# A decoder layer's down projection as seven block products, with its sums made ahead

## The chip, the cores and the metric

One core of one Trainium2 chip runs one decoder layer in single precision. The metric is device time in microseconds for one execution. Engines are named as the profile names them: PE (matrix engine; PEld is its weight load), DVE (vector), ACT (scalar), POOL (GpSimd), SP (the queue that issues nearly all transfers).

## The reference

The layer has a mixer (stick-breaking attention beside gated linear attention), a normalisation, a gated feed-forward with a causal convolution of width 3, and a second normalisation. The change concerns the last product and what follows it:

```python
def conv_glu_ffn(h, w_ff_gate, w_ff_up, conv_w, conv_b, w_down):
    ...
    return (jax.nn.silu(conv) * up) @ w_down          # (2048, 2816) @ (2816, 1024)
...
y = conv_glu_ffn(h, ...)
x = layer_norm(DEEPNORM_ALPHA * x + (1.0 + gate_f) * y, ln2_g, ln2_b)
```

## The kernel before, in words

The 2048 tokens are four tiles of 512 (`TQ`), each of four blocks of 128 (`NB`). A single-precision product is made from three fast matmuls: each operand is split into a rounded part "hi" and a rest "lo", and hi·hi, hi·lo and lo·hi are accumulated. ACT makes the hi part (a cast), DVE or POOL the lo part (a subtraction).

The program has these stages in the order in which they run. The **mixer** (`projections`, `attend`, `gla`, `mixer_out`) mixes PE work with long DVE scans (line 541), POOL products (543) and masks (532, 534). Small left-over jobs are spread over it by `with_ada` (854): a list `ada_todo` of 24 items, one after every fourth yield of `between(t)`; they load through the three buffers `w_raw` of the ring pool. The **feed-forward products** gate and up (`unit`, 1038) use one level of Strassen's form over pairs of token tiles (`t2` = 0 or 1): per unit seven products of 12 matmuls, two column blocks of 128 at a time (index `fp`), 40 units in all and four plain column pairs (`plain`, 1111). The up unit multiplies its result into the gated tile `cv` (two buffers), on POOL for three of the four quarters (1059) and on DVE for one (1078), and stores each half to the DRAM tile `da` (1093). The next gate unit then takes the two `cv` buffers again for its convolution on DVE (1106 to 1108).

The **down projection** (1195 to 1227) is plain: two halves of 512 output columns, in each all 16 token blocks, in each 22 row blocks of 128, and three matmuls for each (`row_wide`, 412). The activations of a block come from `da` one block ahead (`load_a`, 1179), in three parts that go around the buffer pairs `pl`, `gt`, `wsum`, `cv`; the weights of a half stay in the tiles that held the feed-forward's operands. After the first half, the gated sum goes to DRAM (`dr0`) and comes back in the second, where `norm` (383) finishes the rows.

The order on every engine is set by a scheduler that walks the program by priority; `act`, `dve` and `pool` (104) are wrappers that put an operation 300 places ahead. Each engine then runs its list strictly in order.

## Time and profile before

| | us |
|---|---|
| median of 3 runs (2945.28 to 2954.65) | 2952.74 |
| the profiled execution's own time | 2947.66 |
| its span in the profile | 2946.0 |
| busy: PE / DVE / ACT / POOL | 2746.0 / 2013.4 / 1107.6 / 1028.1 |

The span is what lies between the first and the last instruction; the execution's own time has 1.66 us around it. In the stages at the end PE is busy in nearly every slice, DVE about half to three quarters, and POOL stops altogether when the down projection begins.

### The profile page before, as it was taken

How to read it: one execution, taken by the hardware profiler on the slowest of the kernel's cores; microseconds unless marked ns; L12 is line 12 of the kernel's file. 1: busy time of each engine (PE TensorE's matmuls, PEld its weight loads, DVE VectorE, ACT ScalarE, POOL GpSimd, SP SyncE). 2: the span in 40 equal slices, each digit the busy share in tenths (PEclk: the TensorE clock that was granted, in tenths of full speed). 3: DMA queues.
4: the chain of work that ended last, by engine and by line, in shares of the span. 5: the costliest groups of instructions: out<-in, count | busy, mean ns of one | idle time of the engine just before them, and what ended most of it. 6: DMA issues, size and time to landing. Idle time of an engine off the chain costs nothing. (4 is left out here: it accounts for less than half of the span.)

```text
span 2946.0 us, 38134 instructions
## 1 busy us (share of the span) xinstructions
PE 2746.0 (93%) x13387; PEld 2219.7 (75%) x13387; DVE 2013.4 (68%) x2841; ACT 1107.6 (38%) x1870; POOL 1028.1 (35%) x1139
## 2 busy tenths in 40 slices
PE   7989999989999998978979999989999998999998
PEld 6867887777788775656757887867888886888887
DVE  6475567578887789798667767686766665335665
ACT  2442244365656556434223332243223233112111
POOL 2550222155444346375463436462333341000000
PEclk9999999999999998989889999999999999999999
DMA  8978775757684455556784454353322236445553
GB/s 308 361 252 277 256 248 195 229 199 233 204 258 148 143 165 160 172 170 229 265 314 157 122 158 150 115 165 115 86 80 86 79 106 232 130 133 184 167 164 114
DMA packets 370424, 539.62 MB, mean 183 GB/s; under 512 B 25182, under 2 KB 224056, under 8 KB 370232
## 3 DMA queue, kind: packets, MB, share of 16 engines
q1 hardware_dynamic: 368504, 530.89, 55.8%
q0 software_dynamic: 1728, 6.29, 0.6%
q8 instruction: 106, 1.74, 0.2%
q14 instruction: 86, 0.70, 0.1%
HBM read 404.82 MB, written 132.26 MB: 182 GB/s over the span
## 5 line engine op out<-in xcount | busy, mean ns | idle before, releaser
L541 DVE TENSOR_TENSOR_SCAN pp<-pp,beta 128x512 f32<-128x512 f32 (+2 forms) x320 | 384.8, 1218 | 66.4 <-POOL beta L534 37.0
L543 POOL TENSOR_TENSOR beta<-beta,pp 128x512 f32<-128x512 f32 (+2 forms) x160 | 206.2, 1289 | 349.4 <-DVE pp L541 275.0
L101 POOL TENSOR_TENSOR w_lo<-wsum,w_hi 128x1024 fp32r<-128x1024 f32 x80 | 208.2, 2602 | 173.8 <-ACT w_hi L101 173.7
L1017 PE MATMUL acc<-t,w_lo 128*128 128x512 f32 x640 | 247.0, 392 | 9.4 <-DVE w_lo L101 9.3
L1015 PE MATMUL acc<-t,w_hi 128*128 128x512 f32 x640 | 250.2, 393 | 4.4 <-ACT k L1073 2.8
L1016 PE MATMUL acc<-t,w_hi 128*128 128x512 f32 x640 | 249.8, 390 | 0.0
L556 DVE TENSOR_TENSOR wl<-wt,wh 128x512 fp32r<-128x512 f32 (+1 forms) x320 | 186.7, 598 | 82.0 <-ACT wh L555 81.6
L555 ACT CAST wh<-wt 128x512 fp32r<-128x512 f32 (+1 forms) x320 | 162.6, 530 | 201.8 <-PE wt L551 185.9
L529 ACT ACTIVATE pp<-z 128x512 f32<-128x512 f32 (+2 forms) x320 | 173.7, 544 | 121.2 <-PE z L528 81.9
L101 ACT CAST w_hi<-w_raw 128x512 fp32r<-128x512 f32 (+2 forms) x173 | 125.5, 747 | 245.8 <-PE acc L1016 63.6
L292 PE MATMUL acc<-hh,w_hi 128*128 128x512 f32 x480 | 194.5, 406 | 3.8 <-DVE st L101 3.0
L551 PE MATMUL wt<-ident,beta 128*128 128x128 f32 x1088 | 184.2, 286 | 13.8 <-DVE beta L543 8.5
L293 PE MATMUL acc<-hl,w_hi 128*128 128x512 f32 x480 | 192.1, 401 | 0.5 <-DVE hl L101 0.5
L294 PE MATMUL acc<-hh,w_lo 128*128 128x512 f32 x480 | 191.7, 400 | 0.6 <-POOL w_lo L101 0.6
L530 ACT ACTIVATE beta<-z 128x512 f32<-128x512 f32 (+2 forms) x320 | 171.0, 543 | 15.2 <-PE wt L551 15.2
L559 PE MATMUL o_ps<-wl,v 128*128 128x512 f32 (+1 forms) x320 | 133.7, 422 | 43.6 <-DVE wl L556 41.4
L551 PEld LDWEIGHTS wt<-ident,beta 128*128 128x128 f32 x1088 | 139.7, 147 | 44.5 <-DVE beta L543 11.9
L101 DVE TENSOR_TENSOR w_lo<-w_raw,w_hi 128x512 fp32r<-128x512 f32 (+1 forms) x140 | 136.8, 1000 | 53.1 <-ACT w_hi L101 27.5
L527 PE MATMUL z<-k,q 128*128 128x512 f32 (+2 forms) x320 | 137.9, 434 | 16.5 <-ACT beta L530 14.1
L301 PE MATMUL acc<-w_hi,hh 128*128 128x256 f32 (+1 forms) x512 | 148.5, 290 | 1.4 <-ACT w_hi L101 0.7
L1017 PEld LDWEIGHTS acc<-t,w_lo 128*128 128x128 f32 x640 | 120.5, 188 | 37.7 <-DVE w_lo L101 12.3
L302 PE MATMUL acc<-w_lo,hh 128*128 128x256 f32 (+1 forms) x512 | 147.7, 289 | 0.9 <-POOL w_lo L101 0.9
(332 smaller groups left out, 7260.0 us busy)
## 6 DMA issues: line engine op xcount, KB each, us to landing
w_raw<-in_w_ff_gate_dram SPq DMA_DIRECT2D x48, 512.0 KB
w_raw<-in_w_ff_up_dram SPq DMA_DIRECT2D x48, 512.0 KB
k<-dk SPq DMA_DIRECT2D x160, 128.0 KB
v<-dv SPq DMA_DIRECT2D x80, 256.0 KB
da<-cv SPq DMA_DIRECT2D x40, 512.0 KB
w_hi<-dwi_0h SPq DMA_DIRECT2D x39, 512.0 KB
w_lo<-dwi_0l SPq DMA_DIRECT2D x39, 512.0 KB
q<-dq SPq DMA_DIRECT2D x128, 128.0 KB
```

The source lines that it names most:

```text
L101: return f(*args, **kw)
L292: nc.tensor.matmul(ps, hi[:, k % 4, cs], xh[k], start=(k == 0), stop=False)
L293: nc.tensor.matmul(ps, hi[:, k % 4, cs], xl[k], start=False, stop=False)
L294: nc.tensor.matmul(ps, lo[:, k % 4, cs], xh[k], start=False, stop=(k == nk - 1))
L529: nc.scalar.activation(pp[:, 0:n], z[:, 0:n], AF.Sigmoid, scale=-1.0)
L541: nc.vector.tensor_tensor_scan(pp[:, 0:n][:, ::-1], pp[:, 0:n][:, ::-1], beta[:, 0:n], first, ALU.mult, ALU.bypass)
L543: (nc.gpsimd if i in PMU and jt < PMJ else nc.vector).tensor_mul(beta[:, 0:n], beta[:, 0:n], pp[:, 1:n + 1])
L551: pe.transpose(wt[:, i * P:(i + 1) * P], ws[i][:, ks], ident)
L556: nc.vector.tensor_sub(wl[:, cs], wt[:, cs], wh[:, cs])
L1015: nc.tensor.matmul(ps, w[0][:, k, :], t[k][:, 0, :], start=first and k == 0, stop=False, **add)
L1016: nc.tensor.matmul(ps, w[0][:, k, :], t[k][:, 1, :], start=False, stop=False, **add)
L1017: nc.tensor.matmul(ps, w[1][:, k, :], t[k][:, 0, :], start=False, stop=k == 3, **add)
```

## The change

The down projection too is done in one level of Strassen's form. A pair of blocks (block `b` of token tiles 2·t2 and 2·t2+1) gives the two row halves, odd and even row blocks of the weight the two inner halves, and the two halves of 512 columns the two column halves. Eight pairs of blocks and seven products give 56 steps of 11 × 3 matmuls. The products run one after another, each over all eight pairs (`steps`). The results are put together on DVE and ACT in eight tiles `top` (the ring's weight tiles) and eight tiles `low` (operand tiles), so that `dr0` goes.

- **Weight sums.** `sum_w_down(k)`, eleven items at the end of `ada_todo`, taken every second yield: two loads of 512 KB into `w_raw`, three stores of quarters, four POOL subtractions of 128x512 in place, four stores.
- **Activation sums.** `act_sums` after every up unit: four POOL additions or subtractions of 128x512 in the two `cv` tiles, in place, so after their stores to `da`; then four stores to the new DRAM tile `dsa`. The two column pairs that are done by `plain` for the first pair of token tiles are read back and summed by `plain_sums` during later units.
- **Down projection.** Weights come unsplit from DRAM, 11 tiles of 128x512 per product, through 17 tile places; activations come in two parts of 6 and 5 row blocks.

```diff
+    def sum_w_down(k):
+        q = []
+        for j in range(2):
+            raw = wring.tile([P, 1024], F32, name="w_raw", bufs=3)
+            nc.sync.dma_start(raw, w_down[(2 * k + j) * P:(2 * k + j + 1) * P, :])
+            q += [raw[:, 0:512], raw[:, 512:]]
+        b11, b12, b21, b22 = q
+        for d, x in zip(dws[k][4:], (b11, b21, b22)):
+            nc.sync.dma_start(d, x)
+        nc.gpsimd.tensor_sub(b11, b12, b11)
+        nc.gpsimd.tensor_sub(b12, b22, b12)
+        nc.gpsimd.tensor_sub(b22, b22, b11)
+        nc.gpsimd.tensor_sub(b21, b21, b22)
+        for d, x in zip(dws[k], (b11, b12, b22, b21)):
+            nc.sync.dma_start(d, x)
...
-            if cs and i >= ADA0 and i % ADAE == ADAE - 1:
+            n = ADAE if len(cs) > NH else 2
+            if cs and i >= ADA0 and i % n == n - 1:
...
+    ada_todo += [partial(sum_w_down, k) for k in range(NH)]
...
+        if up:
+            act_sums(t2, fp, dst[0][:, A], dst[1][:, A], dst[0][:, B], dst[1][:, B])
+
+    def act_sums(t2, fp, a11, a12, a21, a22):
+        nc.gpsimd.tensor_add(a22, a21, a22)
+        nc.gpsimd.tensor_sub(a21, a11, a21)
+        nc.gpsimd.tensor_sub(a11, a22, a11)
+        nc.gpsimd.tensor_sub(a12, a12, a11)
+        for j, x in enumerate((a22, a11, a21, a12)):
+            nc.sync.dma_start(dsa[t2][:, :, j, fp], x.rearrange("p (b c) -> p b c", c=P))
...
+    def load_w(i, k):
+        w = t_tile(*slots[n_w[0] % NW])
+        n_w[0] += 1
+        raw = w[:, 1, :].bitcast(F32)
+        nc.sync.dma_start(raw, products[i][0](k))
+        act.copy(w[:, 0, :], raw)
+        dve.tensor_sub(w[:, 1, :], raw, w[:, 0, :])
+        return w
...
+    def finish(r, blk, ps, last):
+        t = small()
+        nc.vector.tensor_mul(t, ps, gfb[:, 0:512])
+        nc.vector.tensor_add(r[:, 0:512], r[:, 0:512], t)
+        stats(r, blk, 0)
+        dst = out[blk * P:(blk + 1) * P, :]
+        norm(r, st_all[:, blk], g2b, b2b, nc.vector, m1, (dst[:, 0:512], dst[:, 512:D]) if last else (dst,))
...
+    steps = [(i, b) for i in range(7) for b in range(NP2)]
...
+    for s, (i, b) in enumerate(steps):
+        xh, xl = ahead.pop()
+        if s + 1 < len(steps):
+            ahead.append(load_a(*steps[s + 1]))
+        ps = psm.tile([P, TQ], F32, name="acc", bufs=3)
+        for k in range(NH):
+            w = wset[i][k]
+            nc.tensor.matmul(ps, xh[k], w[:, 0, :], start=k == 0, stop=False)
+            nc.tensor.matmul(ps, xh[k], w[:, 1, :], start=False, stop=False)
+            nc.tensor.matmul(ps, xl[k], w[:, 0, :], start=False, stop=k == NH - 1)
+        if i < 6:
+            if 0 < b < NW - NH + 1:
+                wset[i + 1].append(load_w(i + 1, b - 1))
+            elif b == NP2 - 1:
+                wset[i + 1] += [load_w(i + 1, k) for k in range(NW - NH, NH)]
+        r, blk = top[b], b // NB * 2 * NB + b % NB
+        if i == 0:
+            nc.scalar.copy(r[:, L], ps)
+        elif i == 1:
+            low.append(wide(NW + b))
+            nc.vector.tensor_add(low[b][:, L], r[:, L], ps)
+            nc.scalar.copy(r[:, R], low[b][:, L])
+            gated(r, blk, 0)
+        elif i == 2:
+            nc.vector.tensor_add(low[b][:, L], low[b][:, L], ps)
+        elif i == 3:
+            nc.vector.tensor_add(r[:, R], r[:, R], ps)
+            nc.vector.tensor_add(low[b][:, R], low[b][:, L], ps)
+            gated(low[b], blk + NB, 1)
+            stats(low[b], blk + NB, 1)
+            gated(low[b], blk + NB, 0)
+        elif i == 4:
+            finish(low[b], blk + NB, ps, False)
+        elif i == 5:
+            nc.vector.tensor_add(r[:, R], r[:, R], ps)
+            gated(r, blk, 1)
+            stats(r, blk, 1)
+        else:
+            finish(r, blk, ps, s + 1 == len(steps))
```

(`gated` loads 256 KB of the first normalisation's result, multiplies by the gate and adds: two DVE operations of 128x512; `stats` is one.)

The scheduler moves the instructions. The first place is POOL between two up units of the second pair of token tiles; lines 1059 and 1085 are the product into `cv`, `w_lo<-wsum` makes the lo part of a summed feed-forward weight, 1047 and 1073 copy two columns. Before, three rows of weight work stand behind the last product of a unit:

```order
L1059 TENSOR_TENSOR cv<-cv,k_22150 128x512
L101 TENSOR_TENSOR w_lo<-wsum,w_hi 128x1024
L1059 TENSOR_TENSOR cv<-cv,k_22173 128x512
L101 TENSOR_TENSOR w_lo<-wsum,w_hi 128x1024 x2
L1047 COPY gt<-halo 128x2 x2
L101 TENSOR_TENSOR w_lo<-wsum,w_hi 128x1024
```

And now (1133 to 1136 are the four sums):

```order
L102 TENSOR_TENSOR w_lo<-wsum,w_hi 128x1024
L1085 TENSOR_TENSOR cv<-cv,k_21725 128x512
L1133 TENSOR_TENSOR cv<-cv 128x512
L1134 TENSOR_TENSOR cv<-cv 128x512
L102 TENSOR_TENSOR w_lo<-wsum,w_hi 128x1024
L1135 TENSOR_TENSOR cv<-cv 128x512
L1136 TENSOR_TENSOR cv<-cv 128x512
L102 TENSOR_TENSOR w_lo<-wsum,w_hi 128x1024
L1073 COPY gt<-halo 128x2 x2
```

Two sums stand between the last product and the first of those weight rows, and two behind it.

The second place is POOL in the mixer, in the stage of the third token tile (543 and 565 are the attention's products). Before:

```order
L540 COPY pp<-pp 128x1
L543 TENSOR_TENSOR beta<-beta,pp 128x512
L540 COPY pp<-pp 128x1 x2
L543 TENSOR_TENSOR beta<-beta,pp 128x512
L540 COPY pp<-pp 128x1 x2
L543 TENSOR_TENSOR beta<-beta,pp 128x512
```

And now, at the same place:

```order
L565 TENSOR_TENSOR beta<-beta,pp 128x512
L562 COPY pp<-pp 128x1
L359 TENSOR_TENSOR w_raw<-w_raw 128x512
L360 TENSOR_TENSOR w_raw<-w_raw 128x512
L562 COPY pp<-pp 128x1
L565 TENSOR_TENSOR beta<-beta,pp 128x512
L562 COPY pp<-pp 128x1 x2
```

The weight sums (359 to 362) stand one or two at a time between the attention's rows; all 44 lie between the places of the rows that start at about 834 and 1078 us in the trace of before.

The third place is PE where the down projection begins: the row at which it first needs the buffer pair `cv`. Before:

```order
L420 MATMUL acc_22799<-t5_1_22773,wsum_22708 128x512
L421 MATMUL acc_22799<-t5_0_22772,wsum_22707 128x512
L419 MATMUL acc_22888<-t0_0_22712,cv_22785 128x512
L420 MATMUL acc_22888<-t0_1_22713,cv_22785 128x512
L421 MATMUL acc_22888<-t0_0_22712,cv_22784 128x512
```

And now:

```order
L1306 MATMUL acc_23383<-t1_2_23147,wsum_23330 128x512
L1307 MATMUL acc_23383<-t1_2_23147,wsum_23330 128x512
L1306 MATMUL acc_23236<-t1_2_23147,cv_23187 128x512
L1307 MATMUL acc_23236<-t1_2_23147,cv_23187 128x512
L1308 MATMUL acc_23383<-t1_2_23147,wsum_23329 128x512
L1306 MATMUL acc_23383<-t1_3_23151,wsum_23330 128x512
```

Before, 41 matmuls of the down projection stand between the last one of the feed-forward and this place; now 93 do, because the first parts of later steps (those in `pl`, `wsum` and `gt`) are put ahead.

## Rows read from the trace of the kernel before

**Rows 1.** The page: span, and busy time by engine.

```profile
span 2946.0 us, 38134 instructions
PE 2746.0 (93%) x13387; PEld 2219.7 (75%) x13387; DVE 2013.4 (68%) x2841; ACT 1107.6 (38%) x1870; POOL 1028.1 (35%) x1139
```

**Rows 2.** Windows (stretch, length, busy us by engine, clock, DMA): feed-forward, then both halves.

```profile
2060.00:2440.00 380.00, 376.71 (x1658) 310.69 (x1657) 265.38 (x306) 117.21 (x153) 146.79 (x86) 1.00 0.31 90
2500.00:2600.00 100.00, 100.00 (x443) 82.83 (x442) 36.57 (x41) 19.51 (x20) 0.00 (x0) 1.00 0.45 134
2800.00:2935.00 135.00, 135.00 (x598) 111.81 (x597) 84.93 (x169) 24.30 (x25) 0.00 (x0) 1.00 0.45 145
```

**Rows 3.** Timeline (start, us, engine, line; idle before): the down projection's beginning.

```profile
2453.74 1.28 POOL L1059 TENSOR_TENSOR cv<-cv,k 128x512 f32<-128x512 f32 x1 [3.37 <-DVE k L1058]
2456.47 0.59 SPq L1093 DMA_DIRECT2D da<-cv  x1
2460.86 0.34 SPq L1188 DMA_DIRECT2D cv<-da  x1
2467.97 1.04 ACT L101 CAST cv<-cv 128x1024 fp32r<-128x1024 f32 x1 [0.51 <-DMA cv<-da]
2469.07 0.79 PE L419 MATMUL acc<-t,cv 128*128 128x512 f32 x1 [10.08 <-ACT cv L101]
```

**Rows 4.** Timeline: one load of activations in the first half, issue and cast.

```profile
2561.44 0.32 SPq L1188 DMA_DIRECT2D pl<-da  x1
2565.30 1.05 ACT L101 CAST pl<-pl 128x1024 fp32r<-128x1024 f32 x1 [3.84 <-DMA pl<-da]
```

**Rows 5.** Timeline: DVE for one block of the second half, first to last operation.

```profile
2800.81 0.96 DVE L101 TENSOR_TENSOR cv<-cv 128x768 fp32r<-128x768 f32 x1 [3.79 <-ACT cv L101]
2801.68 0.69 DVE L1220 TENSOR_TENSOR t<-acc,t 128x512 f32<-128x512 f32 x1
...
2805.57 1.23 DVE L101 TENSOR_TENSOR pl<-pl 128x1024 fp32r<-128x1024 f32 x1
...
2808.47 1.29 DVE L395 SCALAR_TENSOR_TENSOR t<-t,rn_rs,t 128x1024 f32<-128x1024 f32 x1
```

**Rows 6.** Timeline: from an up unit's last product to the next convolution.

```profile
2100.90 1.67 POOL L1059 TENSOR_TENSOR cv<-cv,k 128x512 f32<-128x512 f32 x1 [2.00 <-DVE k L1058]
2102.60 0.52 SPq L1093 DMA_DIRECT2D da<-cv  x1
2117.14 0.75 DVE L1106 TENSOR_SCALAR cv<-gt,ccols 128x1024 f32<-128x1024 f32 x1
2117.30 2.85 POOL L101 TENSOR_TENSOR w_lo<-wsum,w_hi 128x1024 fp32r<-128x1024 f32 x1 [6.39 <-ACT w_hi L101]
2117.93 3.31 DVE L1107 SCALAR_TENSOR_TENSOR cv<-gt,ccols,cv 128x1024 f32<-128x1024 f32 x1
2122.95 0.68 DVE L101 TENSOR_TENSOR w_lo<-w_raw,w_hi 128x512 fp32r<-128x512 f32 x1
2130.51 0.50 PE L1017 MATMUL acc<-t,w_lo 128*128 128x512 f32 x1 [0.82 <-DVE w_lo L101]
```

**Rows 7.** Source lines 1107 and 1058, feed-forward of the second pair: ns minimum/median/maximum.

```profile
L1107 DVE SCALAR_TENSOR_TENSOR cv<-gt,ccols,cv x20: 1275/2290/3310, 2076.4 to 2437.0; 128x1024 f32<-128x1024 f32 x20
L1058 DVE TENSOR_TENSOR k<-k,acc x19: 680/687/689, 2062.2 to 2409.3; 128x512 f32<-128x512 f32 x19
```

**Rows 8.** Windows of the mixer: two stretches.

```profile
690.00:830.00 140.00, 132.53 (x773) 107.01 (x773) 120.97 (x157) 82.02 (x165) 69.29 (x109) 0.99 0.71 233
834.00:1078.00 244.00, 232.43 (x1375) 192.00 (x1374) 186.35 (x250) 142.11 (x276) 99.05 (x161) 0.99 0.51 163
```

**Rows 9.** Groups by line: POOL's attention product, 850 to 1110 us.

```profile
L543 POOL TENSOR_TENSOR beta<-beta,pp 128x512 f32<-128x512 f32 x29 | 48.6, 1674 | 98.6 <-DVE pp L541 72.1 <-PE wt L551 8.3 <-PE o_ps L557 4.6
```

**Rows 10.** Timeline: the end, PE's last matmul and the DVE operation behind it.

```profile
2935.21 0.39 PE L421 MATMUL acc<-t,cv 128*128 128x512 f32 x1
2935.63 0.69 DVE L1220 TENSOR_TENSOR t<-acc,t 128x512 f32<-128x512 f32 x1 [7.41 <-PE acc L421]
```

More of the change, by code (lines that the diff above doesn't have):

```diff
@@ L1171, in t_pair, with pairs @@
-    def t_pair(i):
-        return [t_tile(*slots[2 * i + j]).rearrange("p k c -> p (k c)") for j in range(2)]
-    wd = [[], []]
-    for n in range(first, len(units)):
-        unit(n, (0, 1, 3, 4, 2, 5, 6) if n == first else range(7))
-    n_a = [0]
-    def load_a(b):
+    wide = lambda n: t_tile(*slots[n]).rearrange("p k c -> p (k c)").bitcast(F32)
+    def pairs():
+        return [x[:, 512 * i:512 * (i + 1)] for x in
+                [ft.tile([P, WIDTH["pl"]], F32, name="pl", bufs=2) for _ in range(2)] for i in range(2)]
@@ L1181, in load_a @@
+    n_w, n_a = [0], [0]
+    def load_w(i, k):
[6 more added lines that the diff above has]
+        return w
+    def load_a(i, b):
         hi, lo = [], []
-        for f0 in range(0, NFF, 8):
-            n = min(8, NFF - f0)
-            pool, name = ((ft, "pl"), (right["ft2"], "gt"), (ft, "wsum"), (right["ft2"], "cv"))[n_a[0] % 4]
+        src = products[i][1](b)
+        for f0, n in PARTS:
+            pool, name = ((ft, "pl"), (ft, "wsum"), (right["ft2"], "gt"), (right["ft2"], "cv"))[n_a[0] % 4]
@@ L1193, in load_a, with gated @@
         return hi, lo
-    ahead = [load_a(0)]
-    wd[0] += [load_down(0, i, t_pair(i)) for i in range(NFF // 2)]
-    gfb, g2b, b2b = rows = [t_tile(*slots[22 + i]).rearrange("p k c -> p (k c)").bitcast(F32) for i in range(3)]
+    def gated(r, blk, half):
+        ds = slice(half * 512, (half + 1) * 512)
+        x1 = small()
+        nc.sync.dma_start(x1, dx1[blk // NB][blk % NB][:, ds])
+        nc.vector.tensor_mul(r[:, ds], r[:, ds], gfb[:, ds])
+        nc.vector.scalar_tensor_tensor(r[:, ds], x1, ALPHA, r[:, ds], ALU.mult, ALU.add)
@@ new lines, in stats @@
+    def stats(r, blk, half):
+        nc.vector.bn_stats(st_all[:, blk, half, :], r[:, half * 512:(half + 1) * 512])
+    def finish(r, blk, ps, last):
[5 more added lines that the diff above has]
+        norm(r, st_all[:, blk], g2b, b2b, nc.vector, m1, (dst[:, 0:512], dst[:, 512:D]) if last else (dst,))
+    wsums = plain_sums()
+    for n in range(first, len(units)):
+        unit(n, (0, 1, 3, 4, 2, 5, 6) if n == first else range(7))
+        if n >= first + 2:
+            next(wsums, None)
@@ L1198, in layer @@
+    run(wsums)
+    steps = [(i, b) for i in range(7) for b in range(NP2)]
+    ahead = [load_a(0, 0)]
+    wset = [[load_w(0, k) for k in range(NH)]] + [[] for _ in range(7)]
+    gfb, g2b, b2b = rows = [wide(25 + i) for i in range(3)]
     for d, src in zip(rows, (dgate[1], ln2_g, ln2_b)):
         nc.sync.dma_start(d, src.to_broadcast([P, D]))
[L1200 to L1227 removed]
@@ new lines, in layer @@
+    top = [w.bitcast(F32) for _ in range(NP2 // 2) for w in ring_pair()]
+    low = []
+    L, R = slice(0, 512), slice(512, D)
+    for s, (i, b) in enumerate(steps):
[37 more added lines that the diff above has]
+            finish(r, blk, ps, s + 1 == len(steps))
```

72 lines of the change are left out of this document (32 added, 40 removed).

## Prediction

> **What bounds the kernel now.** I read the page's first lines, then the windows of the stages that the change touches, and last the timeline at the places where a buffer changes hands.
>
> The page says that PE is busy 93% of the span and no other engine over 68% [rows 1]. An average hides the stages, so the windows come next [rows 2]. The reader is to see three things. In a stretch of each half of the down projection PE never rests: 443 matmuls in 100 us, 0.2257 us each, at a granted clock of 1.00. In the feed-forward PE is busy 376.7 of 380 us, while DVE has 265 and POOL 147. In the second half of the down projection DVE is at 63% already, POOL at 0. So fewer matmuls are worth their full time, and what is added elsewhere costs only where it makes PE wait. The mixer is less tight: PE 232.4 of 244 us [rows 8].
>
> The sum is made against the profiled execution's own time, 2947.66 us (span 2946.0 and 1.66 around it); that is 0.17% under the median of 2952.74. About 0.3%, 9 us, is what a measurement of this kernel can tell from no change.
>
> **The matmuls.** Removed: 2 halves x 16 blocks x 22 x 3 = 2112. Added: 7 products x 8 pairs x 11 x 3 = 1848, of the same 128x512 form. At 0.2257 us [rows 2] the 264 fewer give **-59.6 us**. A step of 33 matmuls now lasts 7.45 us. The traffic of `dr0` goes too; DMA is at 0.45 there [rows 2] and nothing waits for it, so that is costed at nothing.
>
> **The start of the down projection.** Before, PE idles 10.08 us for the first load that needs `cv` [rows 3]: POOL's product ends at 2455.0, the store goes out at 2456.5, the load 4.4 us later, the cast 7.1 us behind that, the matmul 1.1 us on. The last feed-forward matmul ended about 2469.07 - 10.08 - 41 x 0.2257 = 2449.7. Now four sums of at least 1.28 us (5.1) and another store (up to 4.9, as the first) come in between: 5.3 + 1.5 + 4.4 + 5.1 + 4.9 + 7.1 + 1.1 = 29.4 us behind that matmul. 93 matmuls stand ahead of the place instead of 41, 21.0 us: a gap of 8.4. The load is of half the size and the weight work ahead of it half as much, so I take 6 us, **-4**; bounds -10 (no gap) and +6.
>
> **The activation sums.** Four POOL operations for each of 20 up units, 1.28 to 1.67 us each [rows 3, 6]. POOL has 233 us idle in this window [rows 2], so its share isn't the matter; the buffer is. In [rows 6] the last product ends at 2102.6, its store goes out at once, and the convolution wants `cv` at 2117.14. Now: a store 4.4 us in flight (as in [rows 3]) to 2107.0, two sums to 2109.6, the weight row that the new order puts in between (about 2.4) to 2112.0, two sums to 2114.6, the store's 0.5 and 4.4 to 2119.5. That is 2.4 us late, in each of 11 pairs of units. For the first pair of tiles, where in three of nine pairs more weight work lies between the sums, I take 6 us late. A part comes back: the convolution's 3.31 us in [rows 6] is a slow case of 1.275 to 3.310 [rows 7], beside a POOL row that starts at the same moment, and a later start parts them. From the convolution to the weight's lo part at 2122.95 and PE's wait at 2130.51 there is little slack, so lateness can reach PE. Full: 11 x 2.4 + 9 x 2.4 + 3 x 3.6 = 59; nothing if PE's queue covers it. I take a quarter, **+15**, since the lateness is the size of what the slow convolution gives back; bounds 0 and 59. The stores add 80 issues on SP; a load queued behind a store that waits for sums is late by at most the same few us.
>
> **The weight sums.** 44 POOL operations of the form that takes 1.67 us in the mixer [rows 9], 73 us, in the stretch 834 to 1078, where POOL has 99 of 244 us and DVE 186 [rows 8]. POOL idles 3.4 us ahead of each product (98.6 over 29, most of it on DVE) [rows 9], the time of two sums, and the new order puts one or two into such a place. A sum that starts late in such a gap holds up a product that the scan waits for. 33 stores and 22 loads more, then 44 stores, 30 MB, add about 120 GB/s to 163; the stretch at 233 GB/s ran with PE at 95% [rows 8]. Bounds: 0 if all fit, 73 if none does. I take **+8**, by five gaps in 44 that don't.
>
> **The product switches.** At six of them five weight tiles are free only once the last step of a product has read them: first loaded 0.7 us into that step, first needed 4.1 us into the next, 10.8 us. A load takes 3.9 us to the cast [rows 4], casts and subtractions about 1.3 each, queued five deep. It fits by about 2 us, without margin for a queue on SP. **+3**, bounds 0 and 12 (2 us each).
>
> **The fifth product.** Its result finishes rows. One block's DVE work now runs from 2801.68 to 2809.76, of which 1.23 us is a load's subtraction [rows 5]: 6.85 us remain. The new step adds its own subtractions, 0.96 for six row blocks [rows 5] and some 0.8 for five, and 11/8 weight tiles at 0.68 [rows 6]: 9.5 us against PE's 7.45. Over eight steps the backlog is 17 us; the three accumulators let PE run two steps, 14.9 us, ahead. **+2**, bounds 0 and 17. The other products have less DVE work.
>
> **The end.** Before, 10.4 us lie between PE's last matmul (2935.6) and the end [rows 10]. The seventh product has 8.6 us of DVE work per step, so DVE ends up to 9 us later behind PE: **+6**, bounds 2 and 10.
>
> Sum: -59.6 - 4 + 15 + 8 + 3 + 2 + 6 = -29.6; 2947.7 - 29.6 = **2918 us**.
>
> **The rivals.**
>
> *All of it is hidden.* POOL has room in both stages, and DVE's order is made with buffers in mind. Then only matmuls, start, switches and end remain: -59.6 - 4 + 3 + 6 = -54.6, **2893 us**. Against it: the 2.4 us of lateness worked out from [rows 6]. Chance 0.17.
>
> *POOL and DVE hold each other up in the mixer.* The convolution at line 1107, which reads two tensors from the core's memory, takes 1275 to 3310 ns, while line 1058, whose second input is an accumulator, takes 680 to 689 [rows 7]; and its 3.31 us lie beside a POOL row that itself took 2.85 [rows 6]. If each sum makes a DVE operation wait, up to 73 us go to DVE's 186 of 244, more than the stretch holds; by the 58 us that DVE has free, at least 15 would lengthen it, at most 73. I take 43 in place of 8: **2953 us**, no change from before. Against it: in [rows 8] the earlier stretch ran at DVE 86% and POOL 49% with PE at 95%. Chance 0.12. The Trainium skill ("GPSIMD Engine Reference", section "1. Specifications") says that POOL's interfaces to the core's memory are shared with DVE and contend with DVE instructions that have two inputs there. The trace agrees where it can be read, in the 1275 and 3310 ns of line 1107 against the steady 680 to 689 of line 1058.
>
> *The sums hold the convolution and PE in full* (slower). The place is the convolution's wait for `cv`. If each of 20 pairs costs PE 4.4 us, a whole store's flight, the term is 88 in place of 15: **2991 us**. The point from which it decides is 44.6 us, 2.2 us a pair: there the kernel is as fast as before. For it: PE waits there for the convolution's followers already (0.82 us at 2130.51), and the lateness worked out is just 2.4. Against: DVE has 30% of the window free, and the slow convolution is given back. Chance 0.13.
>
> **How the numbers follow.** The forecast has 0.50, hidden 0.17, the held engines 0.12, the slower case 0.13; 0.08 lies between the forecast and no change. Faster by more than 0.3%, under about 2944: the forecast, the hidden case, and most of what lies between and some of the held engines' low end (15 us: 2925), 0.76. Slower: the slower case and the upper end of the held engines, 0.14. The same: 0.10. The range goes from 2888, the hidden case with no gap at the start, to 2955, where the held engines' case ends; what is left out is the slower case and the corners. The forecast's own range, which takes the feed-forward term from 0 to 30 and the mixer's from 0 to 20, is 2895 to 2945.
>
> **What would show it right or wrong.** Lines 1306 to 1308 should show 1848 matmuls at 0.2257 us, and PE's idle time ahead of them some 6 us at the first `cv` and a few us at each switch. In the feed-forward, the convolution at 1143 should wait for the stores to `dsa`, and PE should lose about 0.75 us a pair; more than 2.2 a pair, and the slower case holds. The mixer's stretch should be 8 us longer; 15 or more, with DVE's rows beside the sums grown, speaks for the held engines. DVE should end the fifth product about two steps behind PE. The prediction fails if the matmuls' 59.6 us don't show, or if a wait that I priced at nothing (ACT's casts, SP's order) ends PE's idle time.

## The result and the profile after

The changed kernel runs in 2909.21 us (median of 4 runs, 2906.14 to 2917.1) against 2949.01 for the one before (2944.34 to 2954.65): a ratio of 0.9867, interval 0.9851 to 0.9883, or 40 us less. The forecast was 2918. The profiled execution took 2910.72 us, 37 less than the one the sum was made against. The page's first lines of the changed kernel, which answer to [rows 1]:

```profile
span 2909.0 us, 38667 instructions
...
PE 2695.8 (93%) x13123; PEld 2176.0 (75%) x13123; DVE 2092.0 (72%) x2984; ACT 1126.2 (39%) x1955; POOL 1206.8 (41%) x1271
```

PE has 264 matmuls and 50 us fewer, POOL 179 us and DVE 79 us more. Where the 37 us come from is told by places that all kernels share: the first and the last matmul of the feed-forward's units, the last matmul of all, and, between the two pairs of token tiles, the first of two matmuls into `z` (line 292 before, 293 after) that wait 0.91 us for a cast. All are starts, in us, read from the trace.

| | before | again | changed | difference to the first |
|---|---|---|---|---|
| first feed-forward matmul (mixer ends) | 1587.4 | 1587.9 | 1594.1 | +6.7 |
| from there to the first `z` wait (first pair) | 410.7 | 412.4 | 424.4 | +13.7 |
| on to the last feed-forward matmul (second pair) | 451.0 | 450.7 | 455.0 | +4.0 |
| on to the last matmul (down projection) | 486.1 | 486.6 | 423.8 | -62.3 |
| on to the end of the span | 10.8 | 10.8 | 11.7 | +0.9 |

The column "again" is a second trace of the kernel before, from the study below: the stages ahead of the down projection repeat within 2 us. The last feed-forward stretch holds 29 matmuls of the down projection now and 25 before, so 0.9 us of its +4.0 belong to the row below it.

The down projection, in windows of the changed kernel (stretch, length, busy us by engine PE, PEld, DVE, ACT, POOL, then clock, DMA share, GB/s); [rows 2] answer to it:

```profile
2520.00:2600.00 80.00, 80.00 (x354) 66.24 (x354) 40.78 (x57) 29.88 (x47) 0.00 (x0) 1.00 0.56 171
2600.00:2700.00 100.00, 100.00 (x443) 82.80 (x442) 62.64 (x90) 32.50 (x47) 0.00 (x0) 1.00 0.53 167
2700.00:2800.00 100.00, 98.83 (x436) 81.51 (x435) 93.54 (x203) 33.41 (x48) 0.00 (x0) 1.00 0.63 210
```

The reader is to see that 443 matmuls still take 100 us: the pitch (the time from one matmul to the next) is the old one, so fewer of them is what counts. DVE reaches 94% in the stretch that holds the fifth product and a part of the sixth, and PE loses 1.2 us there, in the sixth. All of PE's gaps over 0.3 us in the down projection stand in these four rows of the timeline:

```profile
2486.64 0.50 PE L1306 MATMUL acc<-t,wsum 128*128 128x512 f32 x1 [3.66 <-ACT wsum L102]
2493.81 0.51 PE L1306 MATMUL acc<-t,gt 128*128 128x512 f32 x1 [1.41 <-ACT gt L102]
2494.96 0.79 PE L1308 MATMUL acc<-t,gt 128*128 128x512 f32 x1 [0.41 <-DVE gt L102]
2793.16 0.50 PE L1308 MATMUL acc<-t,pl 128*128 128x512 f32 x1 [1.17 <-DVE pl L102]
```

At the start PE idles 5.5 us in place of 10.08 [rows 3], at the six product switches not at all. The start costs more than its idle time, because the matmuls behind it are slow for a while (windows: stretch, length, PE, clock, DMA share, GB/s), in the kernel before and in the changed one:

```profile
2469.00:2473.00 4.00, 3.89 (x8) 0.50 0.94 353
```

```profile
2486.60:2500.00 13.40, 11.36 (x32) 0.75 0.85 275
```

At 0.2257 us these 8 and 32 matmuls would have taken 1.8 and 7.2 us. Counted over the whole start, slow matmuls cost about 3.0 us before and 4.5 now, so the start as a whole is 3 us shorter and not 4.6. The end, answering to [rows 10]:

```profile
2897.33 0.39 PE L1308 MATMUL acc<-t,cv 128*128 128x512 f32 x1
2897.76 0.69 DVE L1277 TENSOR_TENSOR k<-acc,t 128x512 f32<-128x512 f32 x1 [0.17 <-PE acc L1308]
```

DVE takes up the last result at once.

In the feed-forward of the second pair the steady state is better than before. One window, and the convolution's second operation in that pair (minimum, median, maximum in ns), which was 1275/2290/3310 in [rows 7]:

```profile
2206.70:2306.70 100.00, 100.00 (x442) 82.78 (x442) 74.72 (x82) 29.57 (x40) 52.74 (x34) 1.00 0.39 113
```

```profile
L1144 DVE SCALAR_TENSOR_TENSOR cv<-gt,ccols,cv x20: 1270/1283/2199, 2062.0 to 2420.1; 128x1024 f32<-128x1024 f32 x20
```

PE's wait of 0.82 us in every second pair of units [rows 6] is gone there. What the stage lost stands at two places: in the first pair of tiles, and in these two rows at the start of the second:

```profile
2077.39 0.79 PE L1043 MATMUL acc<-t,w_lo 128*128 128x512 f32 x1 [5.08 <-DVE w_lo L102]
2119.34 0.50 PE L1043 MATMUL acc<-t,w_lo 128*128 128x512 f32 x1 [1.45 <-DVE w_lo L102]
```

This gap too costs more than its length. Behind the 5.08 us the granted clock is 0.50, the lower of the two levels (1.2 GHz), and nine matmuls take 3.6 us (windows: stretch, length, PE, clock, DMA share, GB/s):

```profile
2077.40:2081.00 3.60, 3.60 (x9) 0.50 0.82 240
2081.00:2085.00 4.00, 4.00 (x17) 0.88 0.36 112
2085.00:2089.00 4.00, 4.00 (x20) 1.00 0.46 133
```

In the mixer the stretch of [rows 8] now reads:

```profile
834.00:1078.00 244.00, 226.68 (x1322) 186.19 (x1320) 194.75 (x239) 136.09 (x267) 166.55 (x199) 0.96 0.84 281
```

At its start PE was as far as before (4414 matmuls in both); by its end it has done 53 fewer, of which 24 are caught up in the rest of the mixer.

### The profile page after: what moved, and what is told of

It is laid out like the page before. It is cut to its first block, busy times and chain, and to the rows that moved or that the text cites. A ratio compares the mean times of both kernels' runs of the same rounds, so it can differ in the third digit from the quotient of the medians.

```text
span 2909.0 us, 38667 instructions
## 1 busy us (share of the span) xinstructions
PE 2695.8 (93%) x13123; PEld 2176.0 (75%) x13123; DVE 2092.0 (72%) x2984; ACT 1126.2 (39%) x1955; POOL 1206.8 (41%) x1271
## 5 line engine op out<-in xcount | busy, mean ns | idle before, releaser
L563 DVE TENSOR_TENSOR_SCAN pp<-pp,beta 128x512 f32<-128x512 f32 (+2 forms) x320 | 401.5, 1269 | 70.5 <-POOL beta L556 41.7
L565 POOL TENSOR_TENSOR beta<-beta,pp 128x512 f32<-128x512 f32 (+2 forms) x160 | 205.3, 1283 | 291.2 <-DVE pp L563 248.7
L1043 PE MATMUL acc<-t,w_lo 128*128 128x512 f32 x640 | 248.0, 395 | 16.4 <-DVE w_lo L102 16.4
L102 POOL TENSOR_TENSOR w_lo<-wsum,w_hi 128x1024 fp32r<-128x1024 f32 x80 | 204.6, 2558 | 30.4 <-ACT w_hi L102 30.4
L102 ACT CAST w_hi<-wsum 128x1024 fp32r<-128x1024 f32 x80 | 84.0, 1050 | 176.9 <-PE wt L1042 72.8
L102 DVE TENSOR_TENSOR wsum<-w_raw 128x512 f32<-128x512 f32 x80 | 102.8, 1288 | 66.5 <-POOL w_lo L102 54.2
L554 POOL TENSOR_SCALAR_AFFINE_SELECT pp<-pp 128x128 f32<-128x128 f32 x128 | 56.0, 438 | 226.7 <-ACT pp L551 223.1
```

What stands on the lines that cost most here:

```text
L102: return f(*args, **kw)
L563: nc.vector.tensor_tensor_scan(pp[:, 0:n][:, ::-1], pp[:, 0:n][:, ::-1], beta[:, 0:n], first, ALU.mult, ALU.bypass)
L565: (nc.gpsimd if i in PMU and jt < PMJ else nc.vector).tensor_mul(beta[:, 0:n], beta[:, 0:n], pp[:, 1:n + 1])
L1043: nc.tensor.matmul(ps, w[1][:, k, :], t[k][:, 0, :], start=False, stop=k == 3, **add)
```

## The experiments

One of the twelve kernels is the one before, the others are edits of the changed one. The table gives the stages as above, each from one trace; "mixer" is the first feed-forward matmul.

| run | mixer | first pair | second pair | down | median us |
|---|---|---|---|---|---|
| before | 1587.4 | 410.7 | 451.0 | 486.1 | 2949.01 |
| before_again | 1587.9 | 412.4 | 450.7 | 486.6 | 2950.09 |
| changed | 1594.1 | 424.4 | 455.0 | 423.8 | 2909.21 |
| no_prep | 1587.0 | 411.0 | 453.0 | 420.2 | 2886.15 |
| no_act_sums | 1599.4 | 421.2 | 453.1 | 425.9 | 2912.33 |
| no_w_sums | 1592.8 | 423.7 | 454.9 | 420.6 | 2912.33 |
| late_plain | 1598.8 | 421.9 | 454.6 | 422.0 | 2910.98 |
| sums_from_fifth | 1604.5 | 424.7 | 449.9 | 421.2 | 2910.49 |
| sum_order | 1596.7 | 428.8 | 474.9 | 420.3 | 2930.65 |
| sums_no_store | 1621.3 | 426.5 | 472.1 | 421.2 | 2951.74 |
| dsa_on_act | 1598.8 | 426.7 | 452.1 | 424.7 | 2913.89 |
| dsa_on_pool | 1598.4 | 447.9 | 475.8 | 422.0 | 2954.04 |
| w_sums_split | 1606.1 | 423.5 | 455.0 | 424.5 | 2930.02 |
| lean_prep | 1602.6 | 427.4 | 450.8 | 436.3 | 2930.82 |

Six of these (no_act_sums, late_plain, sums_from_fifth, sum_order and both `dsa_on` runs) leave the changed kernel's weight sums as they are; with it their mixers end at 1594.1 to 1604.5, mean 1598.7. So a mixer's end is known to some 5 us from one trace, and differences of 5 us there prove nothing alone; in the first pair two traces of the same order (changed and late_plain, see below) differ by 2.5 us.

One more thing has to be taken off before the last two columns are compared: the stretch of the second pair also holds matmuls of the down projection, 0.2257 us each. There are 25 in the kernel before and in dsa_on_pool, 34 in no_prep, no_act_sums and sum_order, 35 in sums_no_store, none in lean_prep, and 29 or 30 in the others.

**The kernel before once more** (before_again, no edit).

> The kernel before once more, for a second trace of it: in the first one the feed-forward's first matmul came at 1587.3 us and the feed-forward took 862.1 us. The runs so far that share the change's mixer order have that matmul at 1594.0 to 1599.4, and the feed-forward at 875 to 880. Theory A (the mixer and the feed-forward really lost 7 to 12 and 12 to 18 us): the second trace agrees with the first within 3 us in both. Theory B (part of it is the scatter between executions): the first matmul comes at 1590 or later, or the feed-forward takes 866 us or more.

Measured: 1587.9 and 863.1 us (412.4 + 450.7). Theory A: the losses ahead of the down projection are real.

**All preparation left out** (no_prep).

```diff
-        nc.gpsimd.tensor_add(a22, a21, a22)
...
-        for j, x in enumerate((a22, a11, a21, a12)):
-            nc.sync.dma_start(dsa[t2][:, :, j, fp], x.rearrange("p (b c) -> p b c", c=P))
...
-    ada_todo += [partial(sum_w_down, k) for k in range(NH)]
...
-                (lambda k: dws[k][2], partial(act_sum, 1)),
+                ((lambda k: dh[k // KT][k % KT]), partial(act_quarter, 1, 0)),
```

> All that the change adds ahead of the down projection is left out: no weight sums, no activation sums, none of their loads and stores; the seven products read unsummed activations and, as weights, other tiles of the same shape in DRAM. So the down projection has the change's work and order, the stages ahead of it the work of before. Theory A (the mixer's 7 to 11 us and the feed-forward's 12 to 18 us come from the sums with their transfers): first feed-forward matmul at 1586 to 1589 us, feed-forward 862 to 866 us (it holds six matmuls more of the down projection, 1.4 us), down projection 420 to 425, run 2881 to 2887 us. Theory B (part of it comes from something else in the change, the layout of da or the order that the scheduler finds): the feed-forward takes 868 us or more, or the first matmul comes after 1591.

Measured: 1587.0, 864.0 (411.0 + 453.0), 420.2, and 2886.15 us. Theory A, on every number, though the second pair holds nine matmuls more of the down projection than the kernel before, and not six: they are the 2.0 us by which it is longer. The stages ahead lose nothing through the layout of `da` or a scheduler that finds another order by itself; all that they lose comes from the preparation. And the preparation costs 2909 - 2886 = 23 us, so the seven products alone are worth 63.

**The sums of the activations left out, their stores kept** (no_act_sums: the four POOL operations removed), and **the stores left out, the sums kept** (sums_no_store, where also the weight items are spread over the mixer from 100 us on and the raw quarters aren't stored).

> This kernel leaves out the four POOL sums after each up unit and those of the two plain column pairs; their loads and stores stay, so the down projection gets unsummed activations. The feed-forward, from its first matmul (line 1041) to its last, took 879.8 us in the change and 862.1 before. Theory A (the sums cost through POOL: its queue stands still for the store of cv, 77 us over 19 units, and its rows beside DVE's slow these): the feed-forward falls to 858 to 866 us and the run to about 2893 us. Theory B (the 80 stores more, their place in SP's order and the read-back of the plain pairs cost): the feed-forward stays within 875 to 882 us and the run at about 2909 us. The mixer's part (first feed-forward matmul at 1594) should not move by more than 2 us under either.

> Two stages are tried apart. In the feed-forward the POOL sums stand, their stores to dsa are left out (products read unsummed activations). Without sums but with stores it took 874.3 us, with both 876 to 880, before 862.4. If the stores cost most of it: 862 to 869 us here; if sums and stores each cost much the same and only overlap: 872 to 877. In the mixer the 11 weight items stand between the 24 other ones, one after every second, a yield in three, so they run from about 100 us on and not in one piece at 834 to 1078; the raw quarters are not stored (products 1, 6 and 7 take other tiles of the same shape). If the loss in the mixer comes from the crowding of one stage: first feed-forward matmul at 1587 to 1591; if each sum costs the same wherever it stands: 1594 to 1599.

```diff
-        for j, x in enumerate((a22, a11, a21, a12)):
-            nc.sync.dma_start(dsa[t2][:, :, j, fp], x.rearrange("p (b c) -> p b c", c=P))
...
+    jobs = [partial(sum_w_down, k) for k in range(NH)]
+    ada_todo = [f for i, a in enumerate(ada_todo) for f in ([a] + (jobs[i // 2:i // 2 + 1] if i % 2 else []))]
```

Measured: with stores alone the feed-forward took 874.3 us, between both theories; with sums alone 898.6, worse than with both. Neither half carries the loss by itself, and the two don't add. In the first pair of tiles stores alone cost 10.5 us and sums alone 15.8, both together 13.7; in the second pair stores alone cost nothing (451.0 before, and 453.1 with 2.0 us of it in nine more matmuls of the down projection), sums alone 19. One way in which sums cost without their stores is seen in the trace of sums_no_store (1132 is the first sum, `w_lo<-wsum` the lo part of a summed weight):

```profile
2248.06 1.29 POOL L1132 TENSOR_TENSOR cv<-cv 128x512 f32<-128x512 f32 x1 [6.31 <-DMA da<-cv]
2250.67 2.40 POOL L102 TENSOR_TENSOR w_lo<-wsum,w_hi 128x1024 fp32r<-128x1024 f32 x1
2253.11 1.77 DVE L102 TENSOR_TENSOR wsum<-w_raw 128x512 f32<-128x512 f32 x1 [5.63 <-POOL w_lo L102]
```

POOL's lo part stands behind two sums that wait for a store to `da`, and DVE, which needs its buffer, stands still 5.6 us. Over the feed-forward DVE waits so for 82.2 us, against 54.2 in the changed kernel and 28.5 in the one before. That is DVE's idle time, and only a part of it reaches PE, by the place at which it falls: what decides is the order on the in-order queues, and not the amount of work alone. The next runs show other cases. For the mixer the spreading was a miss: 1621.3, the worst of all and outside of both expectations. It is no cure; whether crowding is a part of the changed kernel's loss it doesn't tell.

**Another order of the four sums** (sum_order), the first two written into the buffer that is stored first.

```diff
-        nc.gpsimd.tensor_add(a22, a21, a22)
-        nc.gpsimd.tensor_sub(a21, a11, a21)
-        nc.gpsimd.tensor_sub(a11, a22, a11)
-        nc.gpsimd.tensor_sub(a12, a12, a11)
+        nc.gpsimd.tensor_sub(a11, a11, a21)
+        nc.gpsimd.tensor_add(a21, a21, a22)
+        nc.gpsimd.tensor_sub(a22, a22, a11)
+        nc.gpsimd.tensor_sub(a12, a12, a22)
-        for j, x in enumerate((a22, a11, a21, a12)):
+        for j, x in enumerate((a21, a22, a11, a12)):
```

> The same four activation sums in another order, the first two written into the buffer whose store went out first: a11 - a21 into a11, a21 + a22 into a21, then a22 and a12. In the change POOL waits 4.05 us per unit at the first sum for the store of the second buffer. Theory A (POOL standing still ahead of its weight rows is what costs in the feed-forward): that wait falls under 2 us per unit, the feed-forward shortens by 4 to 10 us, the run to 2899 to 2905 us. Theory B (POOL has time enough, the wait is idle time that costs nothing): the wait falls, and the feed-forward stays within 3 us of 879.8.

Measured: 24 us lost in the feed-forward, where 4 to 10 were to be gained; neither theory foresaw it. With the sums ready earlier the scheduler puts a store to `dsa` ahead of a weight load on SP, and the store waits for the third sum, which waits for the buffer's first store. The timeline of sum_order in the second pair (POOL 1135 is the third sum):

```profile
2144.93 1.29 POOL L1135 TENSOR_TENSOR cv<-cv 128x512 f32<-128x512 f32 x1 [4.64 <-DMA da<-cv]
2146.25 0.51 SPq L1138 DMA_DIRECT2D dsa<-cv  x1
2146.85 0.58 SPq L1012 DMA_DIRECT2D w_raw<-in_w_ff_gate_dram  x1
2151.37 2.35 DVE L102 TENSOR_TENSOR wsum<-w_raw 128x512 f32<-128x512 f32 x1 [6.96 <-DMA w_raw<-in_w_ff_gate_dram]
2166.07 0.50 PE L1043 MATMUL acc<-t,w_lo 128*128 128x512 f32 x1 [2.90 <-DVE w_lo L102]
```

DVE stands still 7 us for a load that SP held back, and PE pays 2.4 to 2.9 us in every second pair of units. In the changed kernel the same load goes out ahead of the stores:

```profile
2135.01 0.37 SPq L1012 DMA_DIRECT2D w_raw<-in_w_ff_gate_dram  x1
...
2136.22 1.29 POOL L1133 TENSOR_TENSOR cv<-cv 128x512 f32<-128x512 f32 x1 [4.39 <-DMA da<-cv]
...
2137.53 7.19 SPq L1138 DMA_DIRECT2D dsa<-cv  x4
```

There the 4.4 us in which POOL stands still ahead of its first sum cost PE nothing.

**The stores on other queues** (dsa_on_pool, dsa_on_act): `nc.sync` in front of the store replaced by `nc.gpsimd` or `nc.scalar`.

> The 80 stores of the activation sums go out from POOL's queue instead of SP's, the rest is the change. Leaving out the sums gave back only 5 us of the feed-forward's 17.7, and another order of the sums, which put two of the stores ahead of a weight load on SP's queue, cost 24 us. Theory A (SP's queue: stores that wait for the sums hold up the loads behind them): with those stores gone from it, the feed-forward falls from 879.8 to 862 to 870 us and the run to about 2898. Theory B (the phase of POOL's rows against the convolution, or the traffic): the feed-forward stays at 876 us or more; POOL's time for 80 issues may make it longer.

> The 80 stores of the activation sums go out from ACT's queue instead of SP's. By the theory of SP's queue the loads are free, but now ACT's casts of the weights stand behind a store that waits for a sum; ACT has 30 of 100 us busy in the feed-forward. SP theory: the feed-forward falls to 862 to 872 us where ACT's order puts the stores behind the casts, and grows above 885 where it puts them ahead. Rival (phase and traffic): 876 to 883 us.

Measured: on ACT's queue the feed-forward took 878.8 us, as on SP's (rival); on POOL's 923.7, and the whole gain was gone (ratio 1.0011, interval 0.9995 to 1.0027). So nothing speaks for SP's queue as what the feed-forward of the changed kernel loses by; its loads go ahead of the stores already. That ACT's queue lost by the stores just what SP's gained is not excluded. What POOL pays for issuing, over the feed-forward of dsa_on_pool (groups by line: count, busy us and mean ns, idle before):

```profile
L1138 POOL DMA_DIRECT2D dsa<-cv x76 | 59.8, 817 | 1.0 <-issue 1.0
L1133 POOL TENSOR_TENSOR cv<-cv 128x512 f32<-128x512 f32 x19 | 24.8, 1305 | 78.2 <-DMA da<-cv 73.9 <-PE acc L1043 4.3
```

Sixty us of issuing stand among the weights' lo parts on POOL. DVE's waits for these grow from 54.2 to 68.5 us, and behind DVE's own lo parts PE waits 30.4 us at line 1043, against 16.4 in the changed kernel. The sums of DVE's waits alone don't show where the 44 us arise: in dsa_on_act DVE waits 70.7 us for POOL's lo parts, at places where PE doesn't feel it.

**Later sums of the plain column pairs** (late_plain: `n >= first + 2` becomes `n >= first + 10`).

> The sums of the two plain column pairs run eight units later, all else is the change. In the change PE waits 5.1 us at 2077 and 1.5 us at 2119 in the first units of the second pair, where these sums stand beside the convolution, and runs some matmuls at half the clock behind the first gap. Theory A (these sums, at a place where DVE has much else, make those gaps): both gaps go, the feed-forward shortens by 6 to 10 us, to about 872 us, and no new gap over 2 us comes eight units later; the run at about 2901 us. Theory B (the gaps come from the start of the second pair itself, or the sums cost the same wherever they stand): the feed-forward stays at 877 to 882 us, the run at about 2909 us.

Measured: nothing moved, the gap of 5.3 us included; but the edit was void. The scheduler issues what is ready, and these sums stood on POOL at the same places as before (2062 to 2090 us). On every engine the order is the changed kernel's, so the run counts as its repetition.

**Sums from the fifth up unit on** (sums_from_fifth).

```diff
+        if fp >= (4 if t2 else CL):
-        nc.gpsimd.tensor_add(a22, a21, a22)
+            nc.gpsimd.tensor_add(a22, a21, a22)
...
```

(`t2` is the pair of token tiles; the plain pairs have `t2` = 0 and `fp` under `CL`.)

> In the second pair of token tiles the POOL sums are left out of the first four up units, and those of the two plain column pairs are left out too; all loads and stores stay, and from the fifth up unit on everything is the change. In the change PE waits 5.1 us at 2077 and 1.5 us at 2119, in the first units of this pair, and then in no unit of it any more, though every unit has its sums. Without any sums (the first run of this study) it waited 1.0 us there and 0.8 in every second pair of units. Theory A (the units slip against PE by some 6 us once, when sums first come in between a unit's products and the next convolution, and from then on the slip is there already and costs nothing): under 1.2 us at about 2077, 0.8 us at most in the pairs without sums, and a gap or two of 4 to 7 us in all about four pairs of units later, at 2220 to 2290; the second pair of tiles takes as long as in the change, within 2 us. Theory B (the sums of the plain pairs, which stand at 2060 to 2088 beside the convolution, make the gap): no gap over 1.2 us anywhere in the second pair of tiles, which takes 5 to 8 us less than in the change. Theory C (each unit's sums cost PE about the same): the wait grows evenly over the units from the fifth on.

Measured: theory B. The waits of PE in the units of the second pair, all over 0.3 us behind the first:

```profile
2084.46 0.50 PE L1043 MATMUL acc<-t,w_lo 128*128 128x512 f32 x1 [1.48 <-DVE w_lo L102]
2161.78 0.50 PE L1043 MATMUL acc<-t,w_lo 128*128 128x512 f32 x1 [0.82 <-DVE w_lo L102]
2239.10 0.50 PE L1043 MATMUL acc<-t,w_lo 128*128 128x512 f32 x1 [0.82 <-DVE w_lo L102]
```

The 5.08 us are gone (1.48 is left, a little over what was expected), and where the units' sums set in, at 2256, there is no gap at all: after 2239.10 PE never waits again in this stage. The second pair took 449.9 us, 5.1 less than in the change (the whole run was no shorter, 2910.49: its mixer ended 10.4 us later). The sums of the units, which I had priced, cost nothing in the steady state; by breaking up the old order they even end the 0.82 us.

The edit takes away two things at the start of the second pair, the plain pairs' sums and the first four units' own. For the 5.08 us the places tell them apart: ahead of 2077 only the four sums of the first plain pair have run, from 2060.14 to 2070.42, and the first unit's own begin at 2098.67. The wait of 1.45 us at 2119 comes behind both, and whose it is stays open. What the four sums do there is to slow DVE. Three of its rows in the changed kernel, then the same three in this run (the convolution's third operation, a weight's lo part, the next convolution's first operation):

```profile
2064.74 2.82 DVE L1145 SCALAR_TENSOR_TENSOR cv<-gt,ccols,cv 128x1024 f32<-128x1024 f32 x1
2067.49 1.78 DVE L102 TENSOR_TENSOR w_lo<-w_raw,w_hi 128x512 fp32r<-128x512 f32 x1
2071.49 2.85 DVE L1143 TENSOR_SCALAR cv<-gt,ccols 128x1024 f32<-128x1024 f32 x1
```

```profile
2076.07 1.28 DVE L1146 SCALAR_TENSOR_TENSOR cv<-gt,ccols,cv 128x1024 f32<-128x1024 f32 x1
2077.26 0.69 DVE L102 TENSOR_TENSOR w_lo<-w_raw,w_hi 128x512 fp32r<-128x512 f32 x1
2079.07 0.76 DVE L1144 TENSOR_SCALAR cv<-gt,ccols 128x1024 f32<-128x1024 f32 x1
```

All three are slowed, also the last, which reads one tensor only. DVE has no idle time in either stretch, and from the first convolution's start to the end of the next one's first operation it takes 13.8 us in the changed kernel and 7.8 here. The difference of 6 us is the size of the gap, so DVE held up by POOL's rows is what the trace shows for it; no run has these sums elsewhere.

**The mixer: POOL's part left out** (no_w_sums: the four subtractions removed, loads and stores kept), **sums one yield behind their loads** (w_sums_split), and **fewer stores** (lean_prep).

> This kernel leaves out the 44 POOL subtractions of the weight sums; all their loads and stores stay, so the down projection gets unsummed weights. The first feed-forward matmul came at 1594.0 us in the change and at 1587.3 before, 6.7 us later. Theory A (POOL's rows cost: they slow DVE's scan, 1326 to 1470 ns, and its product, 852 to 1066 ns, in the stretch 834 to 1078 us): the scan is back at about 1330 ns, the first feed-forward matmul comes at 1586 to 1589, the run at about 2902 us. Theory B (30 MB of traffic and the places on SP's queue cost): the scan may fall, but the first feed-forward matmul stays at 1592 to 1596 and the run at about 2909 us.

> The weight sums are split in two items: loads and stores of the raw quarters first, the four subtractions and their stores one yield later, so that POOL doesn't stand still for loads and stores ahead of the attention's rows (26 us in the stretch 834 to 1078 us of the change). Theory A (that standing still, with the attention's rows behind it, is what the mixer lost): the first feed-forward matmul comes 3 to 7 us earlier than in the change and its kin (1594 to 1599), at 1588 to 1592. Theory B (POOL's rows slow DVE's scan beside them, wherever they stand, or the traffic costs): it stays at 1593 to 1600, and the scan's mean in that stretch stays near 1470 ns.

```diff
+        w_quarters[k] = q
+
+    def sum_w_quarters(k):
+        b11, b12, b21, b22 = w_quarters[k]
...
-            n = ADAE if len(cs) > NH else 2
+            n = ADAE if len(cs) > 2 * NH else 1
...
```

> Two things less to move, the sums as in the change. (1) The raw quarters of the down weight aren't copied to DRAM in the mixer: products 1, 6 and 7 load them from the input through a small tile, so 33 stores fall out of the mixer, and POOL's sums wait for no store of them. (2) The four activation sums leave in two stores of 512 KB in place of four of 256 KB. Of the mixer's loss (first feed-forward matmul 1594 to 1599 in kernels with all of the weight sums, 1592.8 without POOL's part, 1587.6 before), theory A (traffic and places on SP's queue cost about as much as POOL's rows) expects 1590 to 1595; theory B (POOL's rows alone) 1596 to 1599. Of the feed-forward, if the number of stores on SP's queue counts: 870 to 876 us; if not, 877 to 882. The run by the first of both about 2900, by the second about 2911.

```diff
-        for d, x in zip(dws[k][4:], (b11, b21, b22)):
-            nc.sync.dma_start(d, x)
...
-        raw = w[:, 1, :].bitcast(F32)
+        raw = small() if i in (0, 5, 6) else w[:, 1, :].bitcast(F32)
...
+            nc.sync.dma_start(dsa[t2][:, 2 * i:2 * i + 2, :, fp], x.rearrange("p (j b c) -> p j b c", j=2, c=P))
...
```

What POOL's rows do to DVE is plain. The scan and DVE's share of the attention's product, 834 to 1078 us, grouped by line, in the kernel before, in the changed one and in no_w_sums (there the lines have other numbers):

```profile
L541 DVE TENSOR_TENSOR_SCAN pp<-pp,beta 128x512 f32<-128x512 f32 x62 | 80.7, 1326 | 10.7 <-ACT beta L530 8.9 <-POOL beta L534 1.4
L543 DVE TENSOR_TENSOR beta<-beta,pp 128x512 f32<-128x512 f32 x33 | 28.1, 852 | 1.1
```

```profile
L563 DVE TENSOR_TENSOR_SCAN pp<-pp,beta 128x512 f32<-128x512 f32 x60 | 86.7, 1470 | 5.7 <-ACT beta L552 3.2 <-POOL beta L556 2.4
L565 DVE TENSOR_TENSOR beta<-beta,pp 128x512 f32<-128x512 f32 x32 | 34.1, 1066 | 1.9 <-POOL pp L562 1.2
```

```profile
L559 DVE TENSOR_TENSOR_SCAN pp<-pp,beta 128x512 f32<-128x512 f32 x64 | 85.3, 1351 | 16.0 <-ACT beta L548 14.6 <-POOL beta L552 0.8 <-POOL beta L561 0.7
L561 DVE TENSOR_TENSOR beta<-beta,pp 128x512 f32<-128x512 f32 x35 | 30.2, 862 | 1.3
```

With the 44 sums the scan takes 1470 ns in place of 1326, the product 1066 in place of 852: 60 x 0.144 + 32 x 0.214 = 15.5 us more of DVE's time. Without POOL's part, but with all its traffic (DMA share 0.86), both are nearly back. The Trainium skill ("GPSIMD Engine Reference", section "1. Specifications") says that POOL's interfaces to the core's memory are shared with DVE, and that they contend with DVE instructions that have two inputs there; the 1326 and 1470 ns of the scan and the 852 and 1066 of the product agree. How the mixer's loss splits I can't settle: no_w_sums ended it at 1592.8, a number of theory B, while DVE's rows came back as in theory A. That is 5.9 us ahead of the mean of the runs with all weight sums and 5.4 behind the kernel before, so both the rows and the traffic seem to count, but one trace against a scatter of 10 us doesn't show it. Both attempts to ease it were misses. With w_sums_split POOL still waited 27 us for transfers, the scan stood at 1485 ns, the mixer ended at 1606.1, and the run took 2930 us. In lean_prep, with 33 stores fewer, the mixer ended at 1602.6, no better than the others; two stores in place of four gave the feed-forward nothing (878.2); and the first product's weights came late through the small tiles (PE waits 8.2 us there for a cast of `t`). The down projection was 12.5 us longer, of which 6.5 are the 29 matmuls that the changed kernel does in the stretch ahead.

No version that computes everything beat the changed kernel. The experiments point to one version that was not tried: the change with the plain pairs' sums forced to a later place. By sums_from_fifth it would be worth up to 5 us; no run shows it.

## Why the prediction was right, and where it was not

The direction, the size and the range held: 37 us gained in the profiled execution where 29.6 were forecast. By its steps:

- **The matmuls, -59.6.** Right. From the feed-forward's last matmul to the last of all, 62.3 us were saved; 2087 - 1819 = 268 matmuls fewer in it at 0.2257 are 60.5. Less idle time (10.1 to 6.8) and more slow matmuls (3.0 to 4.5) make up the rest.
- **The start, -4.** Right in size (5.5 us idle for 10.08, about -3 with the slow matmuls), wrong in place. The 93 matmuls, with those 5.5 us, were cover enough for `cv`, which made no gap; PE waits for `wsum` instead, whose load went out on SP at 2478.11, behind a store to `da` that waited until 2474.66 for POOL's product, and behind four other transfers. An order on SP that ends PE's idle time was priced at nothing, and the prediction had named it as a sign of failing: its account of the start failed by it, though its sum did not.
- **The activation sums, +15.** The sum was right, +17.7 with 0.9 of the down projection's matmuls in it, and the reasoning wrong; that the two met is luck. The step that failed is the 2.4 us of lateness "in each of 11 pairs of units". The prediction named a sign for it, that the convolution at line 1143 would wait for the stores to `dsa`. Line 1143 over the whole feed-forward, by what ended DVE's idle time (us, times):

```profile
  DMA dsa<-cv: 3.9, 2
```

It waited twice. In the steady state, in the units behind 2131.8, the last store of the buffer that the convolution wants first goes out at 2142.51, the fourth sum, which still reads it, ends at 2144.18, and at 2145.52 the convolution starts when its own input is ready. The store of the fourth sum, out at 2144.21, is of the other buffer, and that one is wanted at 2152.39 only. The step let the convolution wait for this last store too, 4.9 us. So in the second pair that lateness doesn't arise: it was a quarter of 26 us in the term, and the runs show none (sums_from_fifth: no wait behind 2239). The step counted the slow convolution as "given back", and more was: the convolution's second operation is not beside a POOL row any more, median 1283 ns for 2290 (its first operation took on some of it, 2.0 us for 0.75 in every second unit), and the 0.82 us went too. What did cost was what the step had not looked at: the sums for the plain pairs at the start of the second pair (about 5 us, by slowing DVE), and 13.7 us in the first pair, where the units' sums and stores meet the loads and POOL operations of other jobs. Which of these meetings cost how much is open; no_act_sums and sums_no_store show only that either half alone costs 10.5 us or more there.
- **The weight sums, +8.** Right: +6.7 in the profiled execution, +11 as a mean over seven traces.
- **The switches, +3.** Nothing was lost; the margin of 2 us was enough.
- **The fifth product, +2.** PE lost nothing in it; 1.17 us were lost in the sixth, at 2793.16.
- **The end, +6.** Too much: +0.9. Of the last product DVE was busy 54.6 of 60 us for seven blocks, 7.8 a step and not 8.6. The 6.85 us, taken from a block's first operation to its last, held some 0.4 us of gaps between small dependent operations, in which another block's can run; the rest of the difference is not shown.

Of the rivals, *all hidden* (2893) was 16 us off; it is near what no_prep shows, 2886. *The held engines* have the right mechanism and far too high a price: 15.5 us of DVE time and a mixer longer by 7 to 11 us, not 43. The 43 lay between 15, if DVE's free 58 us are used up first, and 73, if each sum holds DVE in full; the rows grew by 15.5 us for some 73 of sums. By its trace the same mechanism made the gap of 5.08 us at the start of the second pair, where the prediction had not looked for it. *The slower case* did not happen in the change, but a loss of its size is near: three other orders of much the same work (sum_order, sums_no_store, dsa_on_pool) make PE wait over many pairs of units, and lose 19 to 44 us in the feed-forward against the change. The place is mostly another one than the prediction's: the convolution's own wait for the stores is 12.0 us in dsa_on_pool and none in the other two; what comes late there are POOL's lo parts and, in sum_order, loads on SP.

## What to carry to other kernels

Fewer matmuls on a bound PE are worth their count times the pitch, and here this part of the sum held; what the added preparation costs is decided by where it falls in the in-order queues, and moved here by 19 to 44 us between orders of much the same work. So read for each added store what load stands behind it, and for each added operation what row of the same engine, before counting busy shares. And a lateness that is worked out once per loop turn isn't to be multiplied by the turns: ask first which of the buffers is wanted when, and whether the engine that sets the pace ever waits for it.

## What was not expected of the hardware

POOL took 817 ns for each DMA that it issued (76 issues, 59.8 us), where the same stores on ACT's queue left the feed-forward at 878.8 us. And the gap of PE of 5.08 us is followed by 3.6 us at half the clock, which adds some 1.7 to its price; behind the 10.08 us at the kernel before's start of the down projection it was about 3.
